# Both parts of a weight half in one buffer and one transfer, and the low-rank factors of the next pair loaded ahead

## The chip, the cores and the metric

The kernel runs on one core of one Trainium2 chip. The metric is the time of one execution on the device in microseconds (us). The kernel before takes 1636.07 us, the median of three runs (1634.64, 1636.07 and 1638.14 us). The engines are called as the profile calls them: PE (matrix multiplications), PEld (its weight loads), DVE (vector), ACT (scalar, activations), POOL (GpSimd) and SP, which here issues every DMA.

## The reference

One layer of a hybrid decoder. A 1024-token prompt and eight sample tokens are projected by one matrix `w_in` of 1024 x 9360 columns; the columns feed a gated linear attention (GLA) branch, an RWKV-7 branch and two gates, and the result is merged, projected and normalised.

```python
p = jnp.einsum('btd,dn->btn', x, w_in)
p_gla, p_rwkv, p_gate = _split(p, (GLA_COLS, RWKV_COLS, GATE_COLS))
o_gla, S_gla = _gla_chunked(q * GLA_DK ** -0.5, k, v, log_a, S_gla0)
...
w = jnp.exp(-RWKV_DECAY_SCALE * jax.nn.sigmoid(rwkv_w0 + jnp.einsum('btr,rc->btc', jnp.tanh(w_lr), rwkv_w2)))
a = jax.nn.sigmoid(rwkv_a0 + jnp.einsum('btr,rc->btc', aa_lr, rwkv_a2))
y, S_rwkv = _rwkv7_scan(r, w, k, v, kk, a, S_rwkv0)
...
m = sigmoid(gate_a) * (o_gla @ w_up_gla) + sigmoid(gate_b) * (o_rwkv @ w_up_rwkv)
y_out = _layernorm(DEEPNORM_ALPHA * x + m @ w_out, ln_g, ln_b, LN_EPS)
```

The low-rank factors `rwkv_w2` and `rwkv_a2` (64 x 1024 each) are the "second low-rank factors" of the change; the kernel gets them as one array `lora2`.

## The kernel before, in words

**Two passes over the tokens.** Pass 0 holds 512 prompt tokens and the eight samples as two tiles of 260 columns, pass 1 the other 512 tokens as one tile. Tokens lie along the free dimension, feature rows along the 128 partitions. Each projection computes a block of 128 output columns: two weight halves of 128 x 512 numbers (half `j` covers four of the eight 128-row slices of `w_in`), and for each slice and tile three matmuls, because values are held as a high and a low part in the fp32r format: high weights by high x, high weights by low x, low weights by high x.

**The weights (`load_w`).** In pass 0 and for the two up-projections a half is loaded as it is (`wraw`), ACT copies the rounded high part into a buffer `whi`, and DVE (or POOL) subtracts to get the low part in `wlo`; four buffers of each. In pass 0 both parts are also stored to DRAM, in two DMAs from `keep`, and in pass 1 they are read back in two DMAs, 146 halves in each pass. Matmuls of `blocks` take pairs (high, low) from the list `ws` and free both buffers after the last slice of the last tile.

**Pairs of RWKV heads (`pair`).** Each pass has eight pairs. A pair runs through `front` (decay and keys from the projected rows), `back` and `turn` (a triangular inverse, transposes), `chain` (eight steps along the sequence, each three matmuls with copies between) and `norm`. In this text pairs are counted through both passes, 0 to 7 in pass 0 and 8 to 15 in pass 1. `front` first takes a buffer `l2s` (there is one), loads the pair's columns of `lora2` into it, splits them into two `l2p` parts, and multiplies them with the low-rank rows `lw`: four matmuls `big<-lw,l2p`. Their results go through ACT (sigmoid) and a long run of DVE work, beginning with the running sum `row<-reset,row` and ending with the tiles `az` and `wide`. PE comes back to the pair with a head sum `big<-part,headsr` and with the matmuls `big<-az,wide`, which need the last of that run.

**What sets the order.** Every instruction is recorded by generators (streams) and one planner, `Order.run`, line 382 and around. At each step it takes, among the streams' next operations, the one with the smallest planned start less a priority, with a cost from `price` for each operation (0.48 us for a DMA issue on SP) and with buffer and data dates of its own. It also chooses the engine where there is a choice. So the order on each engine is fixed when the program is built, and a change in one operation can shift the order of everything behind it. On the chip each engine executes its own list in that order and waits where data is late. All instructions carry the line of the recording helper, L215.

The parts that the change touches are `load_w` with its inner `keep`, `high` and `low`; the use of the halves in `blocks` and at the end of `load_out`; the load of `l2s` at the head of `front`; and the table `WBUF` of buffers.

Of the kernel before, what the change touches and what calls it, by code (L numbers as in the profile page):

```python
# [53 lines left out]
WBUF = {"whi": ([P, 512], 4), "wlo": ([P, 512], 4), "wraw": ([P, 512], 3)}  # L54
# [348 lines left out]
class Kern(Order):  # L403
# [221 lines left out]
    def load_w(self):  # L625

        H = NK // 2
        todo = [(b.src, b.c0, j, b.c.i) for b in self.plan if b.src is not None for j in range(2)]
        raws, his, los, kept = [], [], [], {}

        def keep(src, c0, j, hi, lo):
            for v, x in zip("hl", (hi, lo)):
                t = self.dr.tile([P, 512], F32, name=f"w{v}{c0}_{j}")
                kept.setdefault((c0, j), []).append(t)
                yield self.S.dma_start(t, x.bitcast(F32))

        def high():
            n = 0
            while True:
                yield lambda: len(raws) > n  # L640
                hi = yield from self.get("whi")
                yield self.A.copy(hi, raws[n][0])
                his.append(hi)
                n += 1
                if n == count:
                    return

        def low():
# [12 lines left out]
        self.spawn(high(), "w")  # L661
        self.spawn(low(), "w")
        for n, (src, c0, j, i) in enumerate(todo):
            if src is self.a["w_in"] and i:
                yield lambda: len(los) == len(raws)
                hi, lo = (yield from self.get("whi")), (yield from self.get("wlo"))
                for x, t in zip((hi, lo), kept[c0, j]):
                    yield self.S.dma_start(x.bitcast(F32), t)
                self.ws.append((hi, lo))
                continue  # L670
            raw = yield from self.get("wraw")
            op = self.S.dma_start(raw.rearrange("p (k c) -> p k c", c=P),
                                  src[j * H * P:(j + 1) * H * P, c0:c0 + P].rearrange("(k p) c -> p k c", p=P))
            yield from self.load(f"w{n}", op)
            raws.append((raw, src, c0, j, i))

    def blocks(self):
        xs = None
        for b in self.plan:
# [12 lines left out]
            for tt, (t0, n) in enumerate(tiles):  # L692
# [3 lines left out]
                for k in range(NK):  # L696
# [4 lines left out]
                    hi, lo = (x[:, k % 4 * P:k % 4 * P + P] for x in w[k // 4])  # L701
# [6 lines left out]
                    if fin and k % 4 == 3:  # L708
                        self.free(*w[k // 4])
# [323 lines left out]

    def front(self, c, p, st, d):
# [5 lines left out]
        l2 = yield from self.get("l2s")  # L1040
        yield self.S.dma_start(l2.rearrange("p (q f) -> p q f", q=2), a["lora2"][:, :, p * P:(p + 1) * P])
# [371 lines left out]
    def load_out(self):  # L1413
# [7 lines left out]
        for k in range(NK):  # L1421
# [12 lines left out]
            else:  # L1434
                parts = [(yield from self.get("whi", 2)), (yield from self.get("wlo", 2))]
# [156 lines left out]
    def run_all(self):  # L1592
# [4 lines left out]
        self.plan, self.xq, self.ws, self.wo, self.gts = [], [], [], [], []  # L1597
# [14 lines left out]
        self.spawn(self.load_w(), "w")  # L1612
        self.spawn(samples(), "state")
# [49 lines left out]
```

## Time and profile before

| what | us |
|---|---|
| median of three runs | 1636.07 |
| the profiled execution | 1634.97 |
| its span on the core | 1633.0 |
| PE busy | 1580.9 |
| DVE busy | 1309.8 |
| ACT busy | 880.3 |
| POOL busy | 116.0 |
| mean granted clock of PE | 0.989 of full |

The profiled execution has 2.0 us outside its span and is 1.1 us below the median of the runs. "Busy" is the union of the times of an engine's instructions. Matmuls overlap: one of 260 columns is listed with 290 ns, while the next one starts about 120 ns later, so a PE that is busy is not a PE at its peak, and a pause shorter than the tail of a matmul does not show as idle. A wait shows as idle time in front of an instruction, with the engine or DMA that ended it. The clock that the throttle granted to PE is read from the windows as a share of full speed; in this execution it was below full in four stretches, among them one near 290 us and one near 650 us from the start.

### The profile page before, as it was taken

The numbers are of one execution on the slowest core, as the hardware profiler recorded it, in microseconds if no ns is written. First come the engines' busy times: TensorE is split into PE (matmuls) and PEld (weight loads), VectorE is DVE, ScalarE is ACT, GpSimd is POOL, SyncE is SP. The second block draws the span as 40 slices with busy tenths as digits, with TensorE's granted clock in tenths as the row PEclk, the third lists the DMA queues.
The fourth block names the chain that finished last, engine by engine and source line by source line (L and its number), as shares of the span: only waits on it lengthen the run. The fifth ranks groups of instructions, "written<-read, shape, count | busy, mean of one in ns | idle before, by whom it ended". The sixth has DMA issues, their size and how long they took to land.

```text
span 1633.0 us, 29970 instructions
## 1 busy us (share of the span) xinstructions
PE 1580.9 (97%) x10130; PEld 1404.8 (86%) x10130; DVE 1309.8 (80%) x3396; ACT 880.3 (54%) x2112; POOL 116.0 (7%) x204
## 2 busy tenths in 40 slices
PE   8999999799999998999999999999999999999998
PEld 7899999799999898788888877778878889988786
DVE  7788898889887897679788898989887886656565
ACT  5546766576485757464636472447254758554210
POOL 2100010001000101000000011201000100000000
PEclk9999999899999999999999999999999999999999
DMA  9878775676678556653465446445653577788432
GB/s 292 257 222 251 240 217 157 201 250 191 196 242 264 166 173 210 204 190 120 140 192 161 133 156 200 120 141 178 193 167 117 175 224 253 230 282 270 151 110 84
DMA packets 311924, 315.26 MB, mean 193 GB/s; under 512 B 75363, under 2 KB 197356, under 8 KB 311772
## 3 DMA queue, kind: packets, MB, share of 16 engines
q1 hardware_dynamic: 311772, 313.36, 61.7%
q8 instruction: 80, 1.31, 0.3%
q14 instruction: 72, 0.59, 0.1%
HBM read 195.45 MB, written 117.82 MB: 192 GB/s over the span
## 4 chain that ended last, share of the span: by engine, by line
PE 73%; DVE 14%; DMA 6%; ACT 4%; issue 2%; SPq 1%; POOL 0%; DVEq 0%; POOLq 0%; ACTq 0%
PE proj L215 41%; PE big L215 20%; PE pY L215 7%; PE pch L215 4%; DVE row L215 4%; DVE wide L215 2%; DMA wide<-LD 2%; ACT row L215 1%; DVE X L215 1%; SPq L215 1%; DVE az L215 1%; DMA wraw<-w_in 1%; DVE wlo L215 1%; DVE Xt L215 1%; ACT wide L215 1%
## 5 line engine op out<-in xcount | busy, mean ns | idle before, releaser
L215 PE MATMUL proj<-xh,whi 128*128 128x260 f32 (+1 forms) x1880 | 618.2, 329 | 1.1 <-DVE row L215 0.7
L215 PE MATMUL proj<-xl,whi 128*128 128x260 f32 (+1 forms) x1880 | 617.6, 328 | 0.2 <-DVE xl L215 0.2
L215 PE MATMUL proj<-xh,wlo 128*128 128x260 f32 (+1 forms) x1880 | 616.6, 328 | 0.7 <-POOL wlo L215 0.5
L215 PEld LDWEIGHTS proj<-xh,whi 128*128 128x128 f32 x1880 | 356.6, 190 | 28.5 <-issue 2.6
L215 PEld LDWEIGHTS proj<-xh,wlo 128*128 128x128 f32 x1880 | 356.2, 189 | 26.3 <-issue 2.1
L215 PEld LDWEIGHTS proj<-xl,whi 128*128 128x128 f32 x1880 | 356.4, 190 | 24.8 <-issue 2.6
L215 DVE TENSOR_TENSOR wlo<-wraw,whi 128x512 fp32r<-128x512 f32 x204 | 141.4, 698 | 42.7 <-ACT whi L215 40.3
L215 ACT CAST whi<-wraw 128x512 fp32r<-128x512 f32 x210 | 129.1, 620 | 81.4 <-PE proj L215 34.7
L215 DVE TENSOR_TENSOR row<-row 128x512 f32<-128x512 f32 (+9 forms) x317 | 158.7, 504 | 7.7 <-ACT row L215 3.0
L215 ACT ACTIVATE row<-row 128x512 f32<-128x512 f32 (+5 forms) x229 | 138.3, 611 | 32.5 <-DVE row L215 17.6
L215 DVE TENSOR_TENSOR Xt<-X,wide 128x60 f32<-128x60 f32 (+24 forms) x496 | 104.9, 212 | 31.2 <-DMA wide<-LD 20.5
L215 DVE TENSOR_TENSOR X<-X,Xt 128x60 f32<-128x60 f32 (+24 forms) x496 | 108.2, 218 | 11.4
L215 PE MATMUL big<-row 128*128 128x64 f32 (+4 forms) x712 | 115.0, 278 | 2.1 <-DVE X L215 1.2
L215 ACT ACTIVATE s0p<-wide,pc 64x64 f32<-64x64 f32 x256 | 88.0, 344 | 49.4 <-DVE wide L215 45.4
L215 PEld LDWEIGHTS big<-row 128*128 128x128 f32 (+1 forms) x712 | 97.1, 191 | 7.4 <-DVE row L215 2.7
L215 ACT COPY wide<-pch 64x64 f32<-64x64 f32 x221 | 45.6, 206 | 107.0 <-PE pch L215 103.0
L215 ACT ACTIVATE row<-proj,omu 128x260 f32<-128x260 f32 (+1 forms) x99 | 54.1, 546 | 89.8 <-PE proj L215 84.0
L215 POOL TENSOR_TENSOR row<-row 128x512 f32<-128x512 f32 (+7 forms) x52 | 60.0, 1156 | 560.8 <-DVE row L215 204.5
L215 DVE SCALAR_TENSOR_TENSOR row<-proj,pv,row 128x259 f32<-128x259 f32 (+1 forms) x99 | 56.4, 570 | 34.4 <-ACT tail L215 18.5
L215 ACT COPY wide<-wide 32x256 f32<-32x256 f32 x181 | 73.0, 403 | 18.1 <-DVE wide L215 16.0
L215 DVE SCALAR_TENSOR_TENSOR wide<-pch,pc,s0p 64x64 f32<-64x64 f32 x224 | 63.0, 281 | 21.1 <-PE pch L215 16.8
L215 ACT COPY row<-big 128x128 f32<-128x128 f32 (+7 forms) x162 | 45.4, 309 | 49.1 <-PE big L215 47.4
(259 smaller groups left out, 2770.0 us busy)
## 6 DMA issues: line engine op xcount, KB each, us to landing
wraw<-w_in SPq DMA_DIRECT2D x146, 256.0 KB
wh<-whi SPq DMA_DIRECT2D x146, 256.0 KB
wl<-wlo SPq DMA_DIRECT2D x146, 256.0 KB
whi<-wh SPq DMA_DIRECT2D x146, 256.0 KB
wlo<-wl SPq DMA_DIRECT2D x146, 256.0 KB
wide<-LD SPq DMA_DIRECT2D x64, 128.0 KB
wraw<-w_up_gla SPq DMA_DIRECT2D x32, 256.0 KB
wraw<-w_up_rwkv SPq DMA_DIRECT2D x32, 256.0 KB
```

Source lines behind the costliest of these rows:

```text
L215: ways.append((eng, lambda call=call: call(out, *args, **kw), price(eng, name, out, args, ins)))
```

## The change

Both parts of a half now lie in one buffer `wpart` of 128 x 2 x 512 numbers, four of them. In pass 0 one DMA stores both parts to DRAM after the low part has been computed; in pass 1 one DMA reads both. `load_l2` is a stream of its own: as soon as the single `l2s` buffer is free it loads the factors of the next pair, and `front` takes them from a list.

```diff
-WBUF = {"whi": ([P, 512], 4), "wlo": ([P, 512], 4), "wraw": ([P, 512], 3)}
+WBUF = {"wpart": ([P, 2, 512], 4), "wraw": ([P, 512], 3)}
...
-        def keep(src, c0, j, hi, lo):
-            for v, x in zip("hl", (hi, lo)):
-                t = self.dr.tile([P, 512], F32, name=f"w{v}{c0}_{j}")
-                kept.setdefault((c0, j), []).append(t)
-                yield self.S.dma_start(t, x.bitcast(F32))
-
         def high():
...
-                hi = yield from self.get("whi")
-                yield self.A.copy(hi, raws[n][0])
-                his.append(hi)
+                w = yield from self.get("wpart")
+                yield self.A.copy(w[:, 0], raws[n][0])
+                his.append(w)
...
         def low():
...
-                lo = yield from self.get("wlo")
+                w = his[n]
                 raw, src, c0, j, i = raws[n]
-                yield self.E.tensor_sub(lo, raw, his[n].bitcast(F32))
+                yield self.E.tensor_sub(w[:, 1], raw, w[:, 0].bitcast(F32))
                 self.free(raw)
-                los.append(lo)
+                los.append(w)
                 if src is self.a["w_in"] and i == 0:
-                    yield from keep(src, c0, j, his[n], lo)
-                self.ws.append((his[n], lo))
+                    kept[c0, j] = self.dr.tile([P, 2, 512], F32, name=f"w{c0}_{j}")
+                    yield self.S.dma_start(kept[c0, j], w.bitcast(F32))
+                self.ws.append(w)
...
-                hi, lo = (yield from self.get("whi")), (yield from self.get("wlo"))
-                for x, t in zip((hi, lo), kept[c0, j]):
-                    yield self.S.dma_start(x.bitcast(F32), t)
-                self.ws.append((hi, lo))
+                w = yield from self.get("wpart")
+                yield self.S.dma_start(w.bitcast(F32), kept[c0, j])
+                self.ws.append(w)
...
+    def load_l2(self):
+
+        yield lambda: "cst" in self.has
+        for _ in self.ctx:
+            for p in range(NPAIR):
+                l2 = yield from self.get("l2s")
+                yield self.S.dma_start(l2.rearrange("p (q f) -> p q f", q=2), self.a["lora2"][:, :, p * P:(p + 1) * P])
+                self.l2s.append(l2)
+
     def front(self, c, p, st, d):
...
-        l2 = yield from self.get("l2s")
-        yield self.S.dma_start(l2.rearrange("p (q f) -> p q f", q=2), a["lora2"][:, :, p * P:(p + 1) * P])
+        yield lambda: self.l2s
+        l2 = self.l2s.pop(0)
         l2h, l2l = yield from self.split(l2, "l2p")
         self.free(l2)
```

In `blocks` and `load_out` the two parts are now two slices of one tile instead of two tiles, and `load_l2` is started after `load_w` with the priority of the kind "lora". Because the planner sees other DMAs, the order moves on every engine. Three places follow.

SP's queue where the factors of pair 3 are loaded (`l2s<-lora`; `wh`, `wl` and `w` are the DRAM copies of the parts, `XD` and `XT` tiles of the inverse). Before:

```order
L215 DMA wl_0_3763<-wlo 128x512
L215 DMA wh_1_3837<-whi 128x512
L215 DMA wraw<-w_in 128x4x128
L215 DMA wl_1_3840<-wlo 128x512
L215 DMA wh_0_3941<-whi 128x512
L215 DMA wraw<-w_in 128x4x128
L215 DMA wl_0_3944<-wlo 128x512
L215 DMA l2s<-lora 128x2x128
L215 DMA wh_1_4044<-whi 128x512
```

and the load of the factors of pair 3 now, a whole pair earlier, while pair 2 has just split its own:

```order
L215 DMA gla_s<-row 128x2x256
L215 DMA wraw<-w_in 128x4x128
L215 DMA w_1_2481<-wpart 128x1024
L215 DMA row<-state_gla 128x2x256
L215 DMA row<-vd_2056 128x512
L215 DMA wraw<-w_in 128x4x128
L215 DMA w_0_2546<-wpart 128x1024
L215 DMA l2s<-lora 128x2x128
L215 DMA wraw<-w_in 128x4x128
```

A half now costs SP two issues in pass 0 (raw load, one store) instead of three, and the store waits for the low part.

DVE in the front of pair 3, from the running sum `row<-reset,row` on (`As`, `gg`, `XT`, `X` belong to the `back` of another pair, `wide` with 1024 columns to a `turn`). Before:

```order
L215 SCALAR_TENSOR_TENSOR row<-reset,row 128x512
L215 COPY As_186<-big 32x8x32 x2
L215 SCALAR_TENSOR_TENSOR row<-row,nkk 128x512
L215 TENSOR_SCALAR row<-row,pv,oka 128x512
L215 TENSOR_TENSOR az_177<-row 64x8x64 x2
L215 COPY gg<-az_176 64x8x64 x2
L215 SCALAR_TENSOR_TENSOR row<-row 128x512
L215 TENSOR_TENSOR row<-row 128x512
L215 TENSOR_TENSOR az_177<-row 64x8x64 x2
L215 COPY pc<-row 128x8
L215 TENSOR_TENSOR wide<-row 64x8x64 x4
```

and the last twelve rows of the same run now:

```order
L215 TENSOR_SCALAR row<-row,pv,oka 128x512
L215 TENSOR_TENSOR az_177<-row 64x8x64 x2
L215 SCALAR_TENSOR_TENSOR row<-row 128x512
L215 TENSOR_TENSOR row<-row 128x512
L215 TENSOR_TENSOR az_177<-row 64x8x64
L215 COPY XT_180<-big 32x8x32
L215 STREAM_TRANSPOSE wide<-wide 128x1024
L215 SCALAR_TENSOR_TENSOR row<-proj,pv,row 128x251
L215 SCALAR_TENSOR_TENSOR row<-bnd,pv,row 128x1
L215 SCALAR_TENSOR_TENSOR smp<-shT,pv,row 128x8
L215 STREAM_TRANSPOSE row<-row 128x512
L215 TENSOR_TENSOR wide<-row 64x8x64 x4
```

Transposes of a `turn` and an evacuation of a projection have come in ahead of the last four operations. Between the running sum and these rows there are, besides `row<-row,nkk`, two transposes `X<-XT`, two products and one small one of a GLA head (`row<-row` with 256 and 4 columns), one more evacuation (`row<-proj,pv,row` with 259 columns) and one copy.

PE near the end of pass 0, in the steps of a chain (`pch<-wide,gg`, `pch<-rh`, `pch<-wide` are its three matmuls, each waiting for a copy or product made from the one before). Before:

```order
L215 MATMUL proj<-xh_286,wlo 128x260
L215 MATMUL pch<-rh,XT_180 128x128
L215 MATMUL pch<-wide 128x128
L215 MATMUL pY<-gg,wide 128x128
L215 MATMUL pch<-wide,gg 128x128
L215 MATMUL pY<-az_176,wide 128x128
L215 MATMUL pch<-rh,XT_180 128x128
L215 MATMUL pch<-wide 128x128
L215 MATMUL pY<-gg,wide 128x128
L215 MATMUL pch<-wide,gg 128x128
L215 MATMUL pY<-az_176,wide 128x128
L215 MATMUL big<-part,headsr 128x512 x2
```

and in the same stage now:

```order
L215 MATMUL big<-row 128x256
L215 MATMUL big<-row,wa 16x512 x2
L215 MATMUL pch<-rh,XT_180 128x128
L215 MATMUL big<-row 128x128
L215 MATMUL proj<-xl_283,wpart 128x260
L215 MATMUL proj<-xh_246,wpart 128x260
L215 MATMUL proj<-xh_270,wpart 128x260
L215 MATMUL big<-row,S 128x128
L215 MATMUL big<-row 128x128
L215 MATMUL pch<-wide 128x128
L215 MATMUL big<-row,S 128x128
L215 MATMUL big<-row 128x256
```

Before, the chain's matmuls stood next to each other with nothing of other streams between; now matmuls of a GLA head and of a projection stand between them.

More of the change, by code (lines that the diff above doesn't have):

```diff
@@ L700, in blocks @@
                         w.append(self.ws.pop(0))
-                    hi, lo = (x[:, k % 4 * P:k % 4 * P + P] for x in w[k // 4])
+                    hi, lo = (w[k // 4][:, v, k % 4 * P:k % 4 * P + P] for v in range(2))
                     xh, xl = xs[k]
@@ L708, in blocks @@
                     if fin and k % 4 == 3:
-                        self.free(*w[k // 4])
+                        self.free(w[k // 4])
                 self.spawn(self.evacuate(evac(tt, t0, n, q), ps, b.post if fin else None), "evacuate")
@@ L1434, in load_out @@
             else:
-                parts = [(yield from self.get("whi", 2)), (yield from self.get("wlo", 2))]
+                parts = [[x[:, v] for v in range(2)] for x in (yield from self.get("wpart", 2))]
             for hf in range(2):
@@ L1596, in run_all @@
         self.sampled = self.w_done = False
-        self.plan, self.xq, self.ws, self.wo, self.gts = [], [], [], [], []
+        self.plan, self.xq, self.ws, self.wo, self.gts, self.l2s = [], [], [], [], [], []
         self.setup()
@@ L1612, in run_all @@
         self.spawn(self.load_w(), "w")
+        self.spawn(self.load_l2(), "lora")
         self.spawn(samples(), "state")
```

## The prediction

> **What bounds the kernel now.** I read the page first, then PE's waits, then windows around the longest of them.
>
> ```profile
> span 1633.0 us, 29970 instructions
> PE 1580.9 (97%) x10130; PEld 1404.8 (86%) x10130; DVE 1309.8 (80%) x3396; ACT 880.3 (54%) x2112; POOL 116.0 (7%) x204
> PE 73%; DVE 14%; DMA 6%; ACT 4%; issue 2%; SPq 1%; POOL 0%; DVEq 0%; POOLq 0%; ACTq 0%
> L215 ACT CAST whi<-wraw 128x512 fp32r<-128x512 f32 x210 | 129.1, 620 | 81.4 <-PE proj L215 34.7
> ```
>
> PE is busy for 1580.9 of 1633.0 us, so 52.1 us are idle, and the change takes no matmul away. What it can win are those idle 52 us and the time in which PE's clock is lowered. Who ends PE's waits:
>
> ```profile
> PE big L215 <- ACT part L215: 8.5, 1, 8.5
> PE pch L215 <- DVE wide L215: 7.8, 7, 2.1
> PE big L215 <- DMA row<-xT: 5.1, 2, 4.4
> PE pch L215 <- DVE rh L215: 4.6, 10, 1.3
> PE pch L215 <- ACT wide L215: 2.6, 3, 1.3
> PE big L215 <- DVE l2p L215: 1.9, 1, 1.9
> PE proj L215 <- POOL wlo L215: 0.5, 1, 0.5
> PE proj L215 <- DVE wlo L215: 0.2, 1, 0.2
> ```
>
> (Columns: us in total, times, longest.) Weights are hardly there: 0.7 us for a low part, no row at all for a stored part that is read back. The factors of the change have one row, 1.9 us. The rest is fronts (`part`) and chains (`pch`) that come back to PE too late.
>
> Two stretches hold most of it (columns: length, then busy us of PE, PEld, DVE, ACT, POOL, then PE's granted clock, DMA share, GB/s):
>
> ```profile
> 285.00:290.00 5.00, 3.45 (x30) 3.24 (x29) 4.85 (x9) 4.90 (x10) 0.96 (x1) 1.00 0.93 288
> 290.00:295.00 5.00, 0.00 (x0) 0.00 (x0) 4.96 (x9) 0.91 (x2) 0.32 (x1) 0.54 0.09 34
> 295.00:300.00 5.00, 3.08 (x9) 2.57 (x10) 4.95 (x8) 1.55 (x3) 2.03 (x3) 0.50 0.39 117
> 300.00:305.00 5.00, 5.00 (x21) 4.62 (x21) 3.10 (x5) 3.17 (x8) 0.32 (x3) 0.59 0.63 200
> 640.00:645.00 5.00, 2.79 (x18) 2.04 (x16) 4.69 (x10) 4.35 (x12) 1.39 (x1) 1.00 0.72 259
> 645.00:650.00 5.00, 3.11 (x10) 2.35 (x10) 4.89 (x11) 1.10 (x4) 0.00 (x0) 0.54 0.00 0
> 650.00:655.00 5.00, 4.33 (x14) 2.18 (x13) 4.82 (x10) 3.30 (x8) 2.52 (x6) 0.50 0.36 116
> 655.00:660.00 5.00, 4.78 (x24) 3.45 (x23) 2.34 (x5) 1.23 (x4) 0.00 (x0) 0.94 0.64 202
> ```
>
> The first is the front of pair 3: idle 20 - 11.53 = 8.5 us, then busy time at half clock, 3.08 x 0.50 + 5.00 x 0.41 = 3.6 us lost; together 12.1. The second is the end of pass 0: idle 20 - 15.01 = 5.0, and 3.11 x 0.46 + 4.33 x 0.50 + 4.78 x 0.06 = 3.9 for the clock; together 8.9. In both DVE is busy all the time while PE waits.
>
> [...]
>
> **How long a front needs, and what PE has to do meanwhile.** PE's own rate:
>
> ```profile
> 1335.29 2.88 PE proj L215 x24
> 1447.27 5.57 PE pY L215 x24
> 285.77 1.91 PE L215 MATMUL big<-XT,As 128*128 128x64 f32 x16
> ```
>
> So 0.120 us for a matmul of 260 columns, 0.232 for 512, about 0.11 for each of the two parts of a small one in full fp32. With these I add up the PE work that the order puts between a pair's first `big<-lw,l2p` and its first `big<-az,wide` (the cover). Before: pair 3 13.8 us (61 of 260 columns, 10 of 512, 16 double ones, 4 others), pair 10 21.0, pair 12 27.2, pair 14 19.9, pairs 5, 6, 7 32.4, 32.6, 27.8. The trace shows the same stretches of pairs 3, 10, 12, 14:
>
> ```profile
> 274.98:298.89 23.91, 15.30 (x112) 14.05 (x110) 21.47 (x39) 17.30 (x33) 2.40 (x3) 0.82 0.51 149
> 862.36:883.35 20.99, 20.99 (x109) 17.61 (x108) 20.16 (x37) 15.62 (x31) 2.51 (x7) 1.00 0.49 148
> 1021.35:1052.29 30.94, 28.20 (x137) 22.62 (x138) 30.32 (x56) 14.90 (x31) 9.52 (x12) 1.00 0.47 136
> 1182.24:1202.56 20.32, 20.32 (x97) 16.27 (x97) 19.62 (x47) 10.53 (x20) 3.48 (x7) 1.00 0.60 176
> ```
>
> Where the cover was 20 or 21 us PE never stopped; at 13.8 it stopped for 8.6; at 27.2 it still stopped for 2.7, as DVE had 30.3 us of work in the stretch. A front takes what DVE has in its list, and a cover of 20 is just enough for a short one.
>
> **The change part by part.** The sum is made against the profiled execution, 1634.97 us.
>
> *Transfers.* 146 stores and 146 loads fewer; a store in pass 0 is twice as large and waits for the low part. SP's issue rows (ns min/median/max):
>
> ```profile
> L215 SPq DMA_DIRECT2D wh<-whi x146: 319/382/1746, 9.1 to 651.8; - x146
> L215 SPq DMA_DIRECT2D whi<-wh x146: 319/320/1293, 670.1 to 1299.4; - x146
> ```
>
> That frees 146 x 0.382 + 146 x 0.320 = 102 us of SP. PE's only wait on a DMA in the list above is for `row<-xT` at the start, which the change leaves alone, so the 102 us are worth 0 on the path. The other side: ACT's copy into a buffer must wait until the whole store has landed. ACT already stands 81.4 us before these copies, most of it waiting for PE to leave the buffer, and PE waited 0.7 us for parts; if the store came last each time, those 0.7 us are what would grow. I take 0. Bounds: -0.7, if those waits go, and +3, an estimate of four times their present sum, for pass 0 with its full queues.
>
> *Factors.* The load leaves the front, so the 1.9 us wait before pair 12 goes: -1.9. Nothing is behind it in other fronts, where `l2p` was in time; a front that starts earlier gives PE nothing while it is busy. The new load waits in SP's queue until the split of the pair before is done; behind it stand raw weight loads, three buffers ahead. 0.
>
> *End of pass 0.* The order before put five chain matmuls in a row with no cover; now 1.0 to 2.6 us of other matmuls stand between any two that wait for each other, and chains elsewhere with such spacing have no row of waits over 2.1 us. I take all of it: -8.9. Bounds: -8.9, and 0 if that work is itself late.
>
> *Front of pair 3.* Its cover is now 14.5 us (42 of 260 columns, 10 of 512, 24 double small ones, 12 others), still far under 20. DVE's run from `row<-reset` to the last `wide` gets longer: by these means
>
> ```profile
> L215 DVE STREAM_TRANSPOSE wide<-wide 128x1024 f32<-128x1024 f32 x16 | 19.9, 1245 | 0.2
> L215 DVE STREAM_TRANSPOSE row<-row 128x512 f32<-128x512 f32 x32 | 22.0, 688 | 0.2
> L215 DVE SCALAR_TENSOR_TENSOR row<-proj,pv,row 128x259 f32<-128x259 f32 (+1 forms) x99 | 56.4, 570 | 34.4 <-ACT tail L215 18.5 <-ACT bnd L215 14.3
> L215 DVE STREAM_TRANSPOSE X<-XT 32x256 f32<-32x256 f32 x32 | 13.8, 432 | 2.1 <-DMA XT<-XD 1.4
> L215 DVE COPY gg<-az 64x512 f32<-64x512 f32 x32 | 14.6, 455 | 2.4 <-PE big L215 2.2
> L215 DVE TENSOR_TENSOR az<-row 64x512 f32<-64x512 f32 x62 | 47.9, 773 | 1.3 <-ACT row L215 0.8
> ```
>
> 1.2 + 0.7 + 2 x 0.57 + 2 x 0.43 + 2 x 0.45 (two GLA products, taken like the copies) + about 1.2 for five small ones come in, 2 x 0.46 + 2 x 0.43 + 0.77 + 0.2 go: 6.0 - 2.8 = +3.2. If DVE alone decides, the stall is 8.5 + 3.2 - 0.7 = 11.0; if ACT decides as before, 8.5 - 0.7 = 7.8. I take the middle, 9.4: +0.9, the lowered clock as before.
>
> *Other fronts.* Covers of pairs 5, 6, 7 and 12 fall to 20.6, 21.5, 18.9, 20.5. A front like pair 3's own, 274.98 to its head sum at 274.98 + 21.9, would leave 1.3 + 0.4 + 3.0 + 1.4 = 6.1 us; one like pair 14's none. I take half, 3. Pair 12's old 2.7 are counted within this (kept low for that reason): +3, bounds -2.7 and +6.1 plus a lowered clock.
>
> *Starts of chains.* For pairs 2 and 7 the work between `back`'s last matmul and the chain's first is 7.4 and 8.3 us; the least before was 10.0, for pair 8, without a stop. Bounds 0 and 2.6 + 1.7 = 4.3; taken +2.
>
> *Table loads.* The order has 61 on ACT instead of 49, at
>
> ```profile
> L382 ACT ACT_TABLE_LOAD x48 | 61.6, 1283 | 0.8
> ```
>
> 12 x 1.28 = 15.4 us of ACT, which is idle 46% of the span; where they fall into a front they are part of its length above. 0, at most +5 if a third falls into uncovered fronts.
>
> Sum: -1.9 - 8.9 + 0.9 + 3 + 2 = -4.9, so 1630.1 for an execution like the profiled one, and 1631 with the 1.1 us by which the median of the runs lies above it.
>
> **The rivals.** Differences under 0.2%, 3.3 us, can't be told from no change.
>
> *Fronts turn into stalls* (slower, 0.32). The mechanism is pair 3's: the planner lets PE run out of projections before DVE has finished `wide`. Decided from a cover under 20 us. Price: fronts 6.1 idle, plus 3.6 for the clock in two of them (as after pair 3) = 13.3 instead of 3; pair 3 at 11.0 (+2.5 instead of +0.9); chains 4.3; and the end of pass 0 not mended, since DVE was full there as well (0): 13.3 + 2.5 + 4.3 - 1.9 = +18 at worst; with half of the 8.9 won, +14. I give 1647 (+11) as its middle. For it: covers of four pairs are smaller, and table loads more. Against: pairs 10 and 14 passed with 20 to 21.
>
> *The change does nothing* (1636, 0.13). PE's list holds the same matmuls, and what one stretch wins another gives back. For it: no weight wait worth 1 us exists to be removed. Against: two stretches alone hold 21 us, and the order at one of them is different.
>
> *Pair 3 is mended too* (1621, 0.12). Its factors are there early, so ACT and DVE may reach the long run sooner than the matmuls of the cover are through: another 9.4 us, or 1631 - 9.4 = 1621.6. Against: its cover is no longer than before.
>
> **How the numbers follow.** The forecast, 1631, has 0.43, with a range of its own from 1624 to 1637. Two thirds of that lie under 1632.8 and a quarter within 3.3 us of 1636.07. Faster: 0.28 + 0.12 + 0.03 = 0.43; same: 0.11 + 0.10 = 0.21; slower: 0.04 + 0.32 = 0.36. The range reaches from 1620 (pair 3 mended) to 1648 (the stalls' middle and a little): it leaves out the worst of the stalls and the best sum.
>
> **What would show it.** In the changed kernel's windows from 630 to 670 us PE's idle time should be under 2 us and the clock 1.0. PE's wait for `l2p` should be gone. A stop of 8 to 11 us on `part` or `wide` should stand near 280 us, and stops of 0 to 3 us in the fronts of pairs 5, 6, 7 and 12. SP should show 292 DMAs fewer. I am wrong if PE waits for `wpart`, if a stretch outside these shows a stop over 4 us, or if the clock is lowered in more than three places.

## The result, and the profile after

The changed kernel takes 1644.29 us (median of five runs, 1641.69 to 1651.47); the kernel before took 1635.94 beside it (five runs, 1634.64 to 1638.14). The ratio is 1.0057, with a 95% interval from 1.0031 to 1.0083: slower by 5 to 14 us, where 1631 was forecast. The profiled execution has a span of 1640.7 us against 1633.0, so 7.7 us are to be explained.

The changed kernel's page, its first lines, the chain that ended last, and the two groups that make the parts of a weight:

```profile
span 1640.7 us, 29371 instructions
PE 1584.1 (97%) x10130; PEld 1404.6 (86%) x10130; DVE 1296.3 (79%) x3372; ACT 903.1 (55%) x2142; POOL 118.9 (7%) x210
PE 65%; DVE 18%; DMA 7%; ACT 6%; issue 3%; SPq 2%; POOL 0%; DVEq 0%; POOLq 0%; ACTq 0%
L215 ACT CAST wpart<-wraw 128x512 fp32r<-128x512 f32 x210 | 129.3, 621 | 98.0 <-PE proj L215 46.4
L215 DVE TENSOR_TENSOR wpart<-wraw,wpart 128x512 fp32r<-128x512 f32 x201 | 140.5, 702 | 44.2 <-ACT wpart L215 42.7
```

PE is idle for 1640.7 - 1584.1 = 56.6 us, before 52.1; and its busy time is 3.2 us longer for the same 10130 matmul records. The chain gives DVE 18% instead of 14%: more of the end is set by DVE. Who ends PE's waits now (us in total, times, longest; smaller rows left out):

```profile
PE big L215 <- DVE part L215: 9.5, 6, 7.0
PE pch L215 <- DVE rh L215: 5.9, 9, 1.5
PE big L215 <- DVE row L215: 5.2, 7, 2.1
PE big L215 <- DMA row<-xT: 5.0, 2, 4.6
PE big L215 <- ACT row L215: 3.3, 3, 1.7
PE pch L215 <- DVE wide L215: 2.3, 2, 1.9
PE big L215 <- ACT part L215: 2.2, 1, 2.2
PE big L215 <- DMA row<-lora: 2.0, 1, 2.0
PE proj L215 <- DVE wpart L215: 0.7, 1, 0.7
PE big L215 <- DVE l2p L215: 0.3, 1, 0.3
```

The wait for `l2p` is down from 1.9 to 0.3 and the chains' waits for `wide` from 7.8 to 2.3, both as meant. In their place stand waits of about 2 us: `row` from DVE 5.2 (0.7 before), `row` from ACT 3.3 (0.9), and `row<-lora` 2.0, for a DMA, which PE did not wait for before. A wait of a projection for a weight part still costs 0.7. The two kernels in two stretches, first before, then after (columns as in the prediction's windows):

```profile
0.00:700.00 700.00, 674.66 (x5163) 638.32 (x5164) 585.67 (x1595) 433.48 (x1083) 53.60 (x109) 0.98 0.71 219
700.00:1300.00 600.00, 585.54 (x3135) 489.43 (x3133) 510.37 (x1379) 305.65 (x753) 55.20 (x84) 1.00 0.52 158
```

```profile
0.00:700.00 700.00, 665.87 (x5108) 628.97 (x5109) 575.28 (x1557) 440.64 (x1093) 65.12 (x119) 0.98 0.68 217
700.00:1300.00 600.00, 589.51 (x3148) 491.95 (x3147) 498.10 (x1370) 325.56 (x775) 47.77 (x81) 1.00 0.52 157
```

In the first 700 us, nearly all of pass 0, PE's idle time rises from 25.3 to 34.1 us; in the 600 us behind them it falls from 14.5 to 10.5. The loss is in pass 0, though the largest single gain was expected at its end. The windows there that answer to the prediction:

```profile
285.00:290.00 5.00, 3.20 (x25) 2.56 (x24) 4.94 (x5) 4.10 (x12) 3.65 (x9) 1.00 0.50 161
290.00:295.00 5.00, 0.00 (x0) 0.00 (x0) 4.97 (x11) 4.86 (x13) 0.00 (x0) 0.80 0.00 0
295.00:300.00 5.00, 4.63 (x10) 3.14 (x10) 3.16 (x6) 4.82 (x14) 0.00 (x0) 0.51 0.49 157
465.00:470.00 5.00, 3.21 (x24) 2.70 (x23) 4.94 (x8) 3.53 (x8) 1.83 (x2) 1.00 0.00 0
470.00:475.00 5.00, 4.55 (x18) 4.08 (x19) 5.00 (x7) 0.43 (x2) 2.85 (x2) 0.66 0.85 269
560.00:565.00 5.00, 2.12 (x15) 1.54 (x13) 4.91 (x8) 4.52 (x10) 2.02 (x6) 1.00 0.47 162
565.00:570.00 5.00, 3.34 (x11) 2.47 (x12) 4.89 (x11) 1.11 (x4) 0.53 (x1) 0.61 0.07 6
635.00:640.00 5.00, 2.76 (x24) 2.60 (x23) 4.96 (x11) 2.96 (x8) 0.00 (x0) 1.00 0.00 0
640.00:645.00 5.00, 4.60 (x19) 3.85 (x19) 4.97 (x9) 2.06 (x6) 3.13 (x4) 0.66 0.78 235
```

Near 290 us pair 3 stops much as before (7.0 us instead of 8.5). Near 467, 565 and 638 us stand the fronts of pairs 5, 6 and 7: idle 2.2, 4.5 and 2.6 us, DVE busy in nearly all of it, and the clock lowered behind each.

What PE's longest waits of pass 0 stand in front of, pair 3's aside (start and length in us; the wait is in brackets):

```profile
56.49 1.02 PE L215 MATMUL big<-row 64*8 64x512 f32 x2 [1.95 <-DMA row<-lora]
193.34 0.39 PE L215 MATMUL big<-row 128*128 128x8 f32 x2 [2.08 <-DVE row L215]
469.42 0.50 PE L215 MATMUL big<-part,headsr 128*128 128x512 f32 x1 [1.71 <-ACT row L215]
565.93 0.60 PE L215 MATMUL pch<-wide,gg 128*128 128x128 f32 x2 [1.89 <-DVE wide L215]
639.79 0.49 PE L215 MATMUL big<-part,headsr 128*128 128x512 f32 x1 [2.24 <-ACT part L215]
```

Only the third and the fifth are a front's own head sum. The first two lie in the stretches of the fronts of pairs 0 and 2 but belong to the eight samples: the product with their low-rank factors, which come by DMA, and a product of a GLA head. The fourth is a step of an earlier pair's chain; pair 6's head sum follows at 567.98, right behind DVE's copy for its `part`, so that front was late as well.

**Where along the program the time goes.** The lag of a pair is the time at which its first `big<-lw,l2p` starts, less the PE work that the order puts ahead of it (counted with the prediction's intervals; other intervals shift both rows alike). What it grows by from one pair to the next is lost in that stage, to waits, the clock or slower matmuls.

| lag at pair | 0 | 1 | 2 | 3 | 4 | 5 | 6 | 7 | 8 | 9 | 12 | 15 | end |
|---|---|---|---|---|---|---|---|---|---|---|---|---|---|
| before | 7.3 | 10.0 | 12.4 | 15.1 | 28.1 | 31.7 | 32.8 | 41.0 | 53.4 | 56.0 | 64.7 | 77.7 | 86.9 |
| changed | 5.7 | 13.2 | 16.6 | 23.3 | 37.5 | 39.2 | 46.2 | 56.0 | 63.9 | 65.6 | 74.3 | 85.2 | 94.8 |

("End" is the end of pair 15's chain.) At pair 7 the changed kernel is 15.0 us behind, at pair 8 10.5, at the end 7.9, which is the 7.7 us of the spans. Three questions were put to the chip: is it the edits or the order; where in the order; and what makes a front of pass 0 long.

### The profile page after: what moved, and what is told of

It reads as the page before. It is cut to its first block, busy times and chain, and to the rows that moved or that the text cites. A ratio compares the mean times of both kernels' runs of the same rounds, so it can differ in the third digit from the quotient of the medians.

```text
span 1640.7 us, 29371 instructions
## 1 busy us (share of the span) xinstructions
PE 1584.1 (97%) x10130; PEld 1404.6 (86%) x10130; DVE 1296.3 (79%) x3372; ACT 903.1 (55%) x2142; POOL 118.9 (7%) x210
## 2 busy tenths in 40 slices
DMA packets 269873, 315.22 MB, mean 192 GB/s; under 512 B 70691, under 2 KB 192684, under 8 KB 269724
## 3 DMA queue, kind: packets, MB, share of 16 engines
q1 hardware_dynamic: 269724, 313.34, 60.9%
## 4 chain that ended last, share of the span: by engine, by line
PE 65%; DVE 18%; DMA 7%; ACT 6%; issue 3%; SPq 2%; POOL 0%; DVEq 0%; POOLq 0%; ACTq 0%
PE proj L215 36%; PE big L215 18%; DVE row L215 6%; PE pY L215 6%; PE pch L215 4%; DVE wide L215 3%; ACT row L215 2%; SPq L215 2%; DMA wide<-LD 2%; ACT wide L215 2%; DVE X L215 2%; DVE az L215 1%; DVE wpart L215 1%; DVE Xt L215 1%; ACT L382 1%
## 5 line engine op out<-in xcount | busy, mean ns | idle before, releaser
L215 PE MATMUL proj<-xh,wpart 128*128 128x260 f32 (+1 forms) x3760 | 916.3, 328 | 0.7 <-DVE wpart L215 0.7
L215 PEld LDWEIGHTS proj<-xh,wpart 128*128 128x128 f32 x3760 | 628.9, 190 | 50.5 <-issue 3.0
L215 PE MATMUL proj<-xl,wpart 128*128 128x260 f32 (+1 forms) x1880 | 614.4, 327 | 0.0
L215 PEld LDWEIGHTS proj<-xl,wpart 128*128 128x128 f32 x1880 | 356.7, 190 | 23.4 <-issue 1.7
L215 ACT CAST wpart<-wraw 128x512 fp32r<-128x512 f32 x210 | 129.3, 621 | 98.0 <-PE proj L215 46.4
L215 DVE TENSOR_TENSOR wpart<-wraw,wpart 128x512 fp32r<-128x512 f32 x201 | 140.5, 702 | 44.2 <-ACT wpart L215 42.7
L215 DVE TENSOR_TENSOR row<-row 128x256 f32<-128x256 f32 (+10 forms) x316 | 162.3, 518 | 8.5 <-PE big L215 2.7
L215 ACT ACTIVATE row<-row 128x512 f32<-128x512 f32 (+3 forms) x229 | 138.2, 611 | 26.8 <-DVE row L215 13.8
L215 ACT ACTIVATE s0p<-wide,pc 64x64 f32<-64x64 f32 x256 | 88.1, 344 | 39.9 <-DVE wide L215 35.8
L215 POOL TENSOR_TENSOR row<-row 128x512 f32<-128x512 f32 (+7 forms) x53 | 53.9, 1022 | 657.8 <-DVE Xt L215 175.0
L215 DVE SCALAR_TENSOR_TENSOR wide<-pch,pc,s0p 64x64 f32<-64x64 f32 x224 | 63.0, 281 | 30.9 <-PE pch L215 26.3
L215 PE MATMUL big<-part,headsr 128*128 128x512 f32 x128 | 57.3, 451 | 14.0 <-DVE part L215 9.5
```

The lines of the kernel that those rows point to most:

```text
L215: ways.append((eng, lambda call=call: call(out, *args, **kw), price(eng, name, out, args, ins)))
```

## The edits, or the order

**The order of the kernel before with both edits, and the new order with the old transfers.** In the first the planner's choice at each step is replaced by the list of choices that it made for the kernel before, so PE, DVE, ACT and POOL have that kernel's lists, with merged buffers, merged DMAs and factors loaded a pair ahead. In the second the planner runs as in the changed kernel, but each merged store and load is issued as two DMAs of one part.

```diff
     def run(self):
-        while self.streams:
-            best, before = None, list(self.streams)
+        for n, (sid, eng, skip) in enumerate(PICKS):
...
+            s = next((s for s in self.streams if s.sid == sid), None)
...
+            self.do(s, eng)
```

```diff
-                    yield self.S.dma_start(kept[c0, j], w.bitcast(F32))
+                    yield self.halves(self.S.dma_start(t, w.bitcast(F32)), two, [w[:, v].bitcast(F32) for v in range(2)])
```

> Both edits, but PE, DVE, ACT and POOL get the very list of instructions that they have in the kernel before, and SP's list differs only by the merged transfers and by the place of the sixteen factor loads. Theory A (the loss is in the new order; the transfers cost nothing): 1633 to 1638 us, the wait for l2p near 1020 us gone, the stalls near 290 and 645 us as before. Theory B (the merged store, which waits for the low part, holds up SP and the buffers): 1641 us or more, with PE or ACT waiting for wpart longer than for whi and wlo before.

> The changed kernel's order on PE, DVE, ACT and POOL, but each half is stored and read back in two DMAs of 256 KB, 292 more in SP's list. Theory A: 1641 to 1648 us, like the changed kernel. Theory B: 1639 us or less, since the high part's store need not wait for the low part. A third theory (fewer issues are a gain that the new order hides): 1649 us or more.

Measured: 1637.22 us for the old order with both edits, ratio 1.0007 (0.9997 to 1.0017); 1644.03 for the new order with the old transfers, ratio 1.0049 (1.0030 to 1.0068). The edits in the old order cost nothing that can be measured, and taking the merged transfers out of the new order gives nothing back. (The two DMAs stand next to each other in SP's list, at the place of the merged one, so what comes behind them still waits for the low part.) The whole loss comes with the order: under the old one the same edits cost nothing. In the old order PE still waits for the factors, which theory A had expected to be gone:

```profile
PE big L351 <- ACT part L351: 8.5, 1, 8.5
PE big L351 <- DVE l2p L351: 1.9, 1, 1.9
```

The load is now a pair ahead and the wait is still 1.9 us. So this wait was never one for the load: the split of the factors stands too late in DVE's list, and in the changed kernel it went because the split moved.

**Each edit alone.** The merged buffers and transfers without `load_l2`, and `load_l2` in the kernel before; the planner runs in both.

```diff
-        yield lambda: self.l2s
-        l2 = self.l2s.pop(0)
+        l2 = yield from self.get("l2s")
+        yield self.S.dma_start(l2.rearrange("p (q f) -> p q f", q=2), a["lora2"][:, :, p * P:(p + 1) * P])
```

> Merged buffer and transfers alone, planned anew; the factors are loaded at the head of the front as before. Theory A: anywhere from 1632 to 1655 us, set by the stalls of its own order; PE's waits for wpart under 2 us. Theory B: 1641 to 1647 us, the whole loss.

> Factors a pair ahead alone, planned anew; the weights as before. Theory A: anywhere from 1632 to 1655 us, and the differences of the two single edits do not add up to +8. Theory B: 1634 to 1637 us, as only the wait for l2p of 1.9 us goes.

Measured: 1657.94, ratio 1.0132 (1.0113 to 1.0151), and 1658.9, ratio 1.0143 (1.0124 to 1.0161). Either edit alone loses 21 or 22 us, both together 8; both times lie above the range of either theory. Costs of parts would add; these don't, as draws of an order need not.

**The same kernels with another draw.** The planner's price of a DMA issue is changed by 0.01 or 0.02 us. No instruction's work changes, but PE's lists differ in 54 to 63% of their places.

```diff
     if eng == "S":
-        return 0.48
+        return 0.47
```

> The kernel before with the planner's price of one DMA issue set from 0.48 to 0.47 and nothing else: the same instructions, the same buffers, the same transfers, but the planner's choices fall differently and the order on PE changes over most of the program. Theory (the loss of 8 us is one draw from the planner's orders; the edits themselves are worth nothing, as the old order with both edits showed with 1637.2): the time moves away from 1636 by several us though no work changes, anywhere from 1632 to 1660. Rival (the edits push the planner to worse orders, which the untouched kernel would not get): within 3 us of 1636, 1633 to 1639.

> The kernel before with the planner's price of one DMA issue set to 0.49. Theory (a draw from the planner's orders): 1632 to 1660, unlike the draw with 0.47 by several us. Rival (the edits bias the planner): 1633 to 1639, like the kernel before.

> The changed kernel with the planner's price of one DMA issue set to 0.47. Theory (a draw from the planner's orders): anywhere from 1632 to 1660, with a mean over the two reordered changed kernels like that over the two reordered kernels before. Rival (the edits bias the planner): within 3 us of 1644, and above both reordered kernels before.

> The changed kernel with the planner's price of one DMA issue set to 0.49. Theory (a draw from the planner's orders): 1632 to 1660, unlike the draw with 0.47 by several us. Rival (the edits bias the planner): 1641 to 1647.

> The kernel before, planner's price of a DMA issue 0.46. If the order of the kernel before is a lucky draw and the edits have no bias: 1640 to 1680, and the means of the four redraws of each kernel overlap. If the edits bias the planner: 1640 to 1660, below the redraws of the changed kernel.

> The kernel before, planner's price of a DMA issue 0.50. No bias: 1640 to 1680. Bias: 1640 to 1660, below the redraws of the changed kernel.

> The changed kernel, planner's price of a DMA issue 0.46. No bias: 1640 to 1680, overlapping the redraws of the kernel before. Bias: 1665 to 1690 again.

> The changed kernel, planner's price of a DMA issue 0.50. No bias: 1640 to 1680, overlapping the redraws of the kernel before. Bias: 1665 to 1690 again.

| price | kernel before | ratio | changed kernel | ratio |
|---|---|---|---|---|
| 0.48 | 1635.94 | 1 | 1644.29 | 1.0057 (1.0031 to 1.0083) |
| 0.47 | 1648.92 | 1.0071 (1.0047 to 1.0095) | 1681.46 | 1.0277 (1.0242 to 1.0312) |
| 0.49 | 1656.96 | 1.0129 (1.0096 to 1.0162) | 1676.50 | 1.0247 (1.0219 to 1.0275) |
| 0.46 | 1655.80 | 1.0107 (1.0052 to 1.0161) | 1666.88 | 1.0193 (1.0159 to 1.0226) |
| 0.50 | 1656.16 | 1.0115 (1.0060 to 1.0169) | 1667.12 | 1.0192 (1.0159 to 1.0225) |

All eight redraws are slower than the order that they replace, by 13 to 37 us. Among the planner's draws that were tried, that of the kernel before is the best for its content, and so is that of the changed kernel. The two times of the changed kernel at 0.47 and 0.49 lie above the 1660 that the theory of a draw allowed. The rival did not fall either, though that theory had expected equal means: all four redraws of the changed kernel are above all four of the kernel before, 1673.0 against 1654.5 on the mean, which 1 of 70 ways to deal eight numbers into two fours gives. So the edits probably push this planner toward worse orders as well; by which of its rules was not tried. What one such draw can do, in the changed kernel at a price of 0.47:

```profile
PE big L215 <- DVE part L215: 24.9, 9, 15.9
```

and the window of its longest wait there, all engines and then the small DVE steps with `Xt` alone:

```profile
1345.00:1360.00 15.00, 0.21 (x1) 0.21 (x1) 13.39 (x54) 2.82 (x6) 0.00 (x0) 0.55 0.51 159
1345.00:1360.00 15.00, 10.06 (x47) 0.55 0.51 159
```

PE stands for 15.9 us because DVE's list has the products of a triangular solve, 47 of them and each waiting for the one before, ahead of the one `part` that PE needs. Every operation is the same as elsewhere; one place in a list is not.

## Where in the order

Mixtures of the two orders, with both edits: the list of one order up to a pair's first low-rank matmul, then everything that is left in the sequence of the other.

```diff
+    out = list(R1[:cut])
+    c = Counter(x[0] for x in out)
+    for x in R2:
+        if c[x[0]] > 0:
+            c[x[0]] -= 1
+        else:
+            out.append(x)
```

> Both edits. The order of the kernel before up to pair 9's first low-rank matmul, which is behind the end of pass 0, then what is left in the order of the changed kernel. Theory: the new order is 9.6 us behind the old here and 7.9 at the end, so 1636.4 - 1.7 = 1635, between 1632 and 1638; the difference to the switch at pair 7, 5.4 us, is what the new order wins at the end of pass 0, which the prediction put at 8.9. Rival (the end of pass 0 is worth nothing, and the 7.9 us lie in pass 1): 1629 or less, like a switch at pair 7. Rival (each mixture is a draw of its own): 1640 or more.

> Both edits. The order of the kernel before up to pair 7's first low-rank matmul, from there on what is left in the order of the changed kernel. Theory (the loss of the changed kernel sits in the fronts of pass 0, and the end of pass 0 and pass 1 win): against the PE work done so far the new order is 15.0 us behind the old at this place and 7.9 us at the end, so 1636.4 - 7.1 = 1629, between 1625 and 1633, faster than both kernels. Rival (the loss has no place; each mixture of two orders is a draw of its own): 1637 or more.

> Both edits. The order of the changed kernel up to pair 7's first low-rank matmul, then what is left in the order of the kernel before. Theory (the loss sits in pass 0): 1636.4 + 15.0 = 1651, between 1647 and 1656, slower than both kernels. Rival (the loss has no place): between the two kernels, 1636 to 1645.

| kernel | us | ratio | lag at pair 5 | 6 | 7 | 8 | 9 | end |
|---|---|---|---|---|---|---|---|---|
| old, new from pair 9 | 1634.93 | 0.9995 (0.9984 to 1.0006) | 34.0 | 35.1 | 44.0 | 55.1 | 58.1 | 85.6 |
| old, new from pair 7 | 1639.88 | 1.0016 (1.0003 to 1.0028) | 31.2 | 32.9 | 41.8 | 56.9 | 58.4 | 86.8 |
| new, old from pair 7 | 1669.63 | 1.0219 (1.0197 to 1.0241) | 39.3 | 46.4 | 74.6 | 85.9 | 89.2 | 119.4 |

The switch at pair 9 came out as forecast, 1635: behind pass 0 the new order is no worse than the old (27.5 us of lag from pair 9 to the end, 30.9 in the kernel before). So the loss lies in pass 0. The third row is slow too, as the theory had it, but 19 us more than it said, and that lies at the seam: between pairs 6 and 7 the lag grows by 28.2, against 8.2 and 9.8 in the two whole orders, while from pair 8 on it grows by 33.5 like the old order's own. The switch at pair 7 was a miss: 1639.9 instead of 1629, as the rival (each mixture a draw of its own) had it; its lags are those of an execution of 1634.7 us, the fastest of twelve. What the new order wins at the end of pass 0 did not come along. The front of pair 7 then has 10.6 us of cover and stops:

```profile
PE big L357 <- ACT part L357: 15.4, 2, 8.5
```

(two stops, pair 3's 8.5 and one of 6.9 at pair 7). In the changed kernel the same front has a cover of 18.9, after fronts of pairs 5 and 6 that used 11 to 12 us less cover than before. The gain at the end of pass 0 looks like matmuls saved in the fronts ahead of it; that the one paid for the other fits these numbers and was not shown further.

## What makes a front of pass 0 long

**More matmuls beside pair 3's front.** In the old order 50 projection matmuls (6 us) were to be moved from behind pair 3's front into it.

> The kernel before in its own order, with one thing moved: 50 projection matmuls of 260 columns (6 us of PE work), which PE ran right after pair 3's state products, now stand ahead of the head sum at which PE stopped for 8.5 us. DVE, ACT, POOL and SP keep their order. Theory of the prediction (a front stalls because its cover of 13.8 us is short of the 20 or so that a front needs): the stop shrinks from 8.5 us to about 2.5, the clock is not lowered, and the time falls by 6 to 10 us, to 1626 to 1630. Rival (the weights of those 50 matmuls are cast by the same DVE and ACT that the front waits for, so PE has nothing ready to be covered with): the stop stays, as a wait of a projection for its weights or of the chain behind the front, and the time is 1633 to 1642.

Measured: 1641.60, ratio 1.0036 (1.0024 to 1.0048), slower by some 5 us. But the built program is not the one that the expectation describes. PE's list, before and now, shows all that moved:

```diff
- MATMUL big<-az,wide 128x256 x2
- MATMUL big<-row 128x8 x2
...
- MATMUL big<-az,wide 128x256 x4
...
- MATMUL big<-az,wide 128x256 x2
...
+ MATMUL big<-az,wide 128x256 x2
+ MATMUL big<-row 128x8 x2
+ MATMUL big<-az,wide 128x256 x6
```

The matmuls got ahead of the eight `big<-az,wide`, not of the head sum at which PE stops. At that place the next projection has no buffer for its result: by the planner's own account all 26 of `row` are taken, and two requests wait for one. The order can't place another projection there. The stop is what it was, and the later `az` and `wide` hold up the chain (its longest wait for `wide` 3.1 us):

```profile
PE pch L359 <- DVE wide L359: 10.0, 7, 3.1
PE big L359 <- ACT part L359: 8.5, 1, 8.5
```

So the test of a longer cover did not take place, and it shows what limits this cover: buffers. A kernel with a 27th `row` was not run.

**Less work for DVE.** Both orders with both edits; the low part of a weight is a copy of the raw weight, so the subtraction is left out of the computation, and no list is changed otherwise.

```diff
-                yield self.E.tensor_sub(w[:, 1], raw, w[:, 0].bitcast(F32))
+                yield self.E.tensor_copy(w[:, 1], raw)
```

> Both edits, the order of the kernel before, and the low part of a weight is the raw weight copied instead of raw minus high part: the subtraction is left out. It takes DVE some 0.4 us instead of 0.69 in about 204 places, 50 to 60 us of DVE in all; no engine's list is changed otherwise. Theory (DVE's work decides the fronts of pass 0): each front ends 1 to 2 us earlier, the stops at pairs 3, 6 and 7 shrink, 1625 to 1631 instead of 1637. Rival (steps that wait for one another through ACT, DVE and PE decide; DVE's total doesn't): 1634 to 1640.

> The changed kernel in its own order, with the same subtraction replaced by a copy. Theory (DVE's work decides the fronts of pass 0): the fronts that got shorter covers gain most, 1630 to 1637 instead of 1644, so the new order comes closer to the old. Rival (DVE's total doesn't decide): 1641 to 1647.

Measured: 1630.41 with the old order, ratio 0.9965 (0.9950 to 0.9980), and 1636.15 with the new, ratio 0.9998 (0.9975 to 1.0021): 6.8 and 8.1 us less than the same orders with the subtraction. In the new order the group of 201 went from 702 ns each to

```profile
L357 DVE CAST wpart<-wraw 128x512 fp32r<-128x512 f32 x201 | 86.7, 435 | 24.7 <-PE proj L357 7.9 <-PE big L357 7.3 <-PE pY L357 2.8
```

so 54 us of DVE work are worth 7 to 8 us of time, as the theory had it. Where they were won the traces tell only in part, since the profiled executions are the slowest of ten with the old order (1634.97) and the fastest of ten with the new (1628.72). In the latter, PE's wait for `row<-lora` near 56 us is down from 1.95 to 0.2 us and the stage of pair 0 loses 4.3 us less, of 13.7 us that its lag is smaller at the end:

```profile
SPq L215 <- DVE wpart L215: 8.4, 2, 5.5
SPq L357 <- DVE wpart L357: 1.9, 1, 1.9
PE big L357 <- DMA row<-lora: 0.2, 1, 0.2
```

The first two rows are SP's waits from 44 to 60 us, with the subtraction and without. SP's queue stood at a raw weight load until DVE was done with the low part (49.74 us), then issued the load, a store (1.98 us for the issue) and only then, at 52.60 us, the factors that PE waited for until 56.49. So this part of the loss is a load late in SP's queue, not a front's length.

The long fronts hardly moved: pair 3's stop in the old order is 8.3 instead of 8.5, the fronts of pairs 5 and 6 in the new order take 5.7 and 8.0 us beyond their cover instead of 5.6 and 8.3, and the two orders stay 5.7 us apart where they were 7.1. The reason for the first stands in the windows from 275 to 297.5 us, DVE's weight splits alone and then all engines (old order, with the subtraction):

```profile
275.00:297.50 22.50, 2.66 (x4) 0.81 0.47 140
275.00:297.50 22.50, 14.03 (x107) 13.32 (x105) 20.05 (x36) 16.54 (x31) 1.74 (x2) 0.81 0.47 140
```

DVE works for 20.05 of 22.5 us there, but only 2.66 of it on weights, and ACT's copy to `part`, the one that PE waits for, itself waits for DVE (5.34 us in the trace of the kernel before, whose lists these are): this front is bound by what stands in DVE's list, which the cheaper copy hardly touches. For pairs 5 and 6 in the new order the runs do not settle whether DVE's list or steps that wait for one another decide; DVE was idle for up to 2.7 us at a time in pair 5's.

## Why the prediction was wrong, point by point

By stage, from one pair's first low-rank matmul to the next, the forecast terms beside the difference of the lags (changed less before); the term for other fronts is split as the prediction had it, half of 1.3, 0.4, 3.0 and 1.4:

| stage of pair | forecast | measured |
|---|---|---|
| 0 | 0 | +4.8 |
| 1 | 0 | +1.0 |
| 2 (start of a chain) | +1.0 | +4.0 |
| 3 (its front) | +0.9 | +1.2 |
| 4 | 0 | -1.9 |
| 5 (other fronts) | +0.7 | +5.9 |
| 6 (other fronts) | +0.2 | +1.6 |
| 7 (end of pass 0, front, start of a chain) | -6.4 | -4.5 |
| 8 to 11 (factors: their wait stands just ahead of pair 12) | -1.9 | -0.9 |
| 12 (its front) | +0.7 | -4.3 |
| 13 to the end | 0 | +2.6 |
| sum | -4.8 | +9.5 |

(The sum of the forecasts is the prediction's -4.9 but for rounding. The changed kernel is 1.6 us ahead at the start, so 7.9 remain.)

*The step that failed* is the rule that "a cover of 20 is just enough for a short one", and with it a sum that has terms only where a cover shrank.

The rule was read from pairs 10 and 14, both in pass 1. In the changed kernel pass 1 bears it out: pairs 10 and 12 with covers of 22.0 and 20.5 take 0.5 and 1.3 us beyond them. (The time beyond the cover is that from a pair's first `big<-lw,l2p` to its first `big<-az,wide`, less the cover.) In pass 0 the head sum that PE comes back to started only 22.5, 27.9 and 22.4 us after the first low-rank matmul in pairs 5, 6 and 7, with covers of 20.6, 21.5 and 18.9; beyond these the fronts take 5.6, 8.3 and 4.7 us. The kernel before had it on show already: with covers of 32.6 and 27.8 its pairs 6 and 7 take 5.6 and 10.1 us beyond, and pair 7's head sum started 34.6 us after its first low-rank matmul. Its stretch (columns as in the prediction's windows):

```profile
617.06:655.00 37.94, 32.95 (x219) 28.64 (x219) 28.71 (x60) 30.81 (x71) 6.03 (x10) 0.87 0.61 201
```

So the size of a cover says little in pass 0. Over all 16 pairs the time beyond the cover rose from 39.9 to 48.6 us, by 8.7. That is not all the fronts' own doing: in the stretch of a front PE's list also holds matmuls of other streams, which wait for data of their own, and this the prediction passed over. (It put pair 12's 2.7 us of idle time down to its front, too; 2.1 of them stand ahead of `pch<-wide,gg`, a step of a chain.) In the stage of pair 0 the wait for `row<-lora` and the lowered clock behind it (3.41 us at 0.50, PE busy throughout) make 1.95 + 1.7 = 3.7 of the 4.8 us, and in that of pair 2 the wait of the GLA samples' product, with as long a stretch at 0.50 behind it, 2.08 + 1.7 = 3.8 of the 4.0. The prediction bounded four fronts whose cover shrank and gave the others nothing. Stages 0 to 2 came out 8.8 us worse than forecast, stages 5 to 7 8.5; the rest of the gap between -4.8 and +9.5 is small terms of both signs, among them 5.0 us won in stage 12, where two waits of 2.1 us for a chain's `wide` went.

*Transfers: right.* 0 forecast, 0 measured in both orders; PE waits for weight parts for 1.0 us (0.7 and 0.3) where it was 0.7, and the bound of +3 was not needed. The new wait for a DMA, `row<-lora`, is there with two DMAs a half as well (1.8 us), so it belongs to the order. SP issues 292 DMAs fewer, and that is worth nothing.

*Factors: right in size by luck, wrong in cause.* The wait fell from 1.9 to 0.3, but with the old order it stayed at 1.9 although the load was early: the split's place decided, not the load.

*End of pass 0: mis-sized.* Taken whole at -8.9; the stage gave -4.5 with its other terms, where -6.4 was summed. The clock is lowered there once more (0.66), by a wait of 2.2 us in the front of pair 7, so "idle under 2 us and the clock 1.0" did not come true.

*Front of pair 3: right in the sum, not in the stop.* The stop is 7.0 us, under the 8 to 11 forecast; a wait of 1.1 us at the pair's low-rank matmuls is new, and what the front takes beyond its cover went from 10.1 to 10.4, +0.3 where +0.9 was said.

*Starts of chains: no stop.* In the stages of pairs 2 and 7, which had +2 for it, no matmul of a chain waited for over 0.5 us. The +4.0 of stage 2 is the samples' product named above. No run shows the 1.7 us that the bound of 4.3 adds for a lowered clock: behind none of these starts the clock was lowered, and what it took in stage 2, 1.7 us, came behind the samples' product.

*The clock.* "Lowered in more than three places" was named as a sign of being wrong, and it is lowered in six. It is a small part of the loss: the stretches at half rate, the one at the very end aside, last 27.3 us in all after (3.41, 3.41, 6.83, 3.41, 6.83, 3.41) and 30.7 before (13.7, 6.8, 10.2), but counted as in the prediction, by PE's busy time in them, they lose 12.1 us after and 11.0 before. The loss is idle time, +4.5, and busy time, +3.2, of which the clock is 1.1; what else makes the matmuls take longer was not tried.

*Table loads.* The trace has 12 more, as counted. Three of 1.28 us each start on ACT in the front of pair 5 (449.5 to 462.9 us); what the 12 cost was not tried.

*The rivals.* The time, 1644, lies near the rival "fronts turn into stalls" (1647), and its direction was right. Its mechanism was half right: the stops in the fronts of pairs 5 to 7 are there, but the longest of each is 1.7 to 2.2 us, the end of pass 0 was mended in part, and the waits in the stages of pairs 0 and 2 were in no rival.

## What to carry to other kernels

Where a planner sets the order, an edit of the operations is first of all a new draw of the order: price the edits in the old order, and expect a replanned kernel to lose what was good in the old draw, here 8 to 46 us in all eleven replans. Before using work of one engine as cover for another, ask what buffers that work needs to start; a cover that has no buffer for its result cannot be moved. Before idle time in a stretch is put down to what the stretch is named after, look at the instruction that it stands in front of. A rule for stalls read in one stage (one tile a block) should be applied to another stage only after it has been tried on a stall there.

## What the runs showed of the hardware

In the changed kernel PE's clock was at half behind several waits of about 2 us: one of 1.95 us, for `row<-lora` near 56 us, is followed by 3.41 us at 0.50 from 57.53 us on, and others of 2.08 and 2.24 us, near 193 and 640 us, and of 1.71 us with 0.54 right behind it, near 469 us, likewise, from 194.06, 641.21 and 470.54 us on. Two of them in windows:

```profile
55.00:60.00 5.00, 3.51 (x14) 2.65 (x15) 3.28 (x5) 1.13 (x3) 0.00 (x0) 0.75 0.88 319
190.00:195.00 5.00, 2.92 (x20) 2.67 (x19) 4.67 (x12) 4.94 (x11) 0.00 (x0) 0.91 0.33 79
```

All lowered stretches of the two traces, the one at the very end of each aside: in the changed kernel from 57.53, 194.06, 293.05, 470.54, 566.11 and 641.21 us on, for 3.41, 3.41, 6.83, 3.41, 6.83 and 3.41 us; in the kernel before from 290.40, 542.98 and 645.38 us on, for 13.65, 6.83 and 10.24 us. In each of the two traces the starts lie whole multiples of 3.413 us apart (40, 29, 52, 28 and 22 of them; 74 and 30). Not every wait of about 2 us has such a stretch behind it: in the kernel before the clock stayed at 1.00 after waits of 2.13 and 2.06 us near 1049 and 1070 us, and in the changed kernel after one of 1.70 us near 858, while in the kernel before 1.18 us near 542 were followed by 6.83 us at half. What makes the difference was not shown. Where PE was busy for all of a stretch of 3.41 us at 0.50, it lost 1.7 us to it, so the wait for `row<-lora` cost about 2 + 1.7 us. In the kernel before, near 290 us, PE stood from 288.45 us, and the clock was at half from 290.40 us, 1.95 us into a wait of 8.47.

Storing and reading both parts of a half in one DMA took the packets of the queue from 311772 to 269724 for the same 313.3 MB, and its share of the engines' time from 61.7% to 60.9%; under the old order no time came of it (ratio 1.0007).
